# A matrix product with layer norm: the first quarter opened over four k tiles only, its sums put aside, and B's first pieces on a second queue

## The chip, the cores and the metric

The kernel runs on one core of one Trainium2 chip. A core has TensorE (PE, the matrix unit, with its weight loads shown as PEld), VectorE (DVE), ScalarE (ACT), GpSimd (POOL) and SyncE (SP), which run their own instruction lists in order and wait for each other by semaphores. Transfers are asked for by a queue (SP's, ScalarE's or GpSimd's) and done by 16 DMA engines. Matmul results go to PSUM, which holds eight banks of 128 partitions x 512 float32; everything else on the core lies in SBUF.

The metric is the device time of one execution in microseconds (us). Before the change it was 251.15 us, the median of three runs (250.21, 251.15, 252.37).

## The reference

```python
# a: 2048 x 2048, b: 2048 x 2048, gamma, beta: 2048, all float32; eps = 1e-5
x = np.matmul(a, b)
mean = np.mean(x, axis=-1, keepdims=True)
var = np.var(x, axis=-1, keepdims=True)
normalized = (x - mean) / np.sqrt(var + eps)
return (gamma * normalized + beta).astype(np.float32)
```

Each output row is normed over all 2048 columns, so a row can be finished only when all its columns are summed.

## The kernel before

**Tiles.** The 2048 rows of A are 16 row tiles of 128, the contraction is 16 k tiles of 128 (four chunks of four), and the columns are four quarters of 512. One matmul takes a 128 x 128 piece of A, transposed, as weights and a 128 x 512 piece of B; 16 of them, one per k tile, add up one bank: a row tile's quarter. There are 16 x 4 x 16 = 1024 matmuls (`mm`, line 86). Inputs are cast from float32 to float16 by VectorE; B stays in SBUF for the whole run.

**Opening.** The first R = 7 row tiles are worked on together while the input arrives. Pieces of 256 KB come in the order of the list `arrivals`: for chunk 0, A of row 0, B of k tile 0, A of row 1, B of k tile 1 and so on, then A of rows 4 to 6; for each later chunk, A of two rows and then a B tile. `load_piece` (lines 178 to 196) issues each on SP's queue into half of a staging buffer (tag `st`, six buffers of 512 KB) and has VectorE cast it. `turn` (lines 214 to 222) transposes a row's chunk on TensorE, four transposes of 128 x 128 per row, into one PSUM bank (two rows share a bank from chunk 1 on), and ScalarE copies the result to the tile `at`. `emit` hands out matmuls of quarter 0 between the transposes, as their A and B become known, and `filler` (line 212) puts in matmuls on zeros. Quarter 0's seven sums stay in seven banks over all four chunks, which leaves the eighth for transposes.

**First and second quarter.** Lines 280 to 284 finish quarter 0 row by row: ScalarE copies a bank to the row's tile `x` and VectorE takes its statistics (`evacuate`, lines 91 to 97). Then quarter 1 of all seven rows runs with the k tile outermost (lines 286 to 293), its last four k tiles row by row. B's remaining quarters come by `load_b2` (lines 198 to 203) in pieces of two k tiles, 512 KB, which `bring` places between the other work. VectorE runs its list in the order written, so where a `bring` stands sets what its cast waits behind.

**The rest.** From line 359 rows go one by one: rows 0 to 6 have quarters 2 and 3 left, rows 7 to 15 all four. When a row's last quarter is in, `stats` makes mean and root, and `queue_norm` puts the row's norm into `backlog` in two pieces of two quarters; `drain` places pieces between the evacuations. The norm is two VectorE passes per quarter (lines 112 and 118), then a store on SP's queue (line 124). A of rows 7 to 15 is loaded with a cast on GpSimd's queue (line 305), behind a copy (`gate`, line 276) that waits for the last B tile, and transposed by a DMA that SP issues at row i for row i + 5 (line 365). The last row has a shortened tail (`finish_row`).

Which tile uses which buffer follows from pools: `st` has six buffers, `a16` (A cast, not yet transposed) three, `at` four pairs of rows, `x` seven rows, and `ps` the eight PSUM banks. A new tile waits until the old one in its buffer has been read for the last time.

Of the kernel before, what the change touches and what calls it, by code (L numbers as in the profile page):

```python
# [9 lines left out]
FP32 = mybir.dt.float32  # L10
FP16 = mybir.dt.float16
AluOp = mybir.AluOpType
# [4 lines left out]
def kernel(  # L17
# [9 lines left out]
    nc = tc.nc  # L27
    P = 128
    M, K = a.shape
    K2, N = b.shape  # L30
    assert K == K2
    n_mt = M // P
    n_kt = K // P
    NB = 512
    n_nb = N // NB
    NH = N // 2
    KC = 4
    KW = KC * P
    n_kc = n_kt // KC
    R = 7  # L40
    early, e_cap, p_cap = 4, 3, 7
    n_row = n_mt - R
    assert n_kt % KC == 0 and n_nb == 4 and R % 2 == 1 and n_row >= 5

    if isinstance(eps, bass.AP):
        eps_ap, eps_val = eps, None
# [20 lines left out]
    b16 = bpool.tile([P, n_kt, N], FP16)  # L67

    pair = {}
    xs = [None] * n_mt  # L70
    bnst = [None] * n_mt
# [8 lines left out]
    def at(i):  # L80
        return pair[i // 2][:, i % 2]

    def mm(i, q, kt, first, last):
        if (i, q) not in acc:
            acc[i, q] = bank(f"acc{i}_{q}")
        nc.tensor.matmul(  # L86
            acc[i, q], at(i)[:, kt, :], b16[:, kt, ds(q * NB, NB)],
            start=first, stop=last,
        )

    def evacuate(i, q):
        if xs[i] is None:
            xs[i] = xpool.tile([P, N], FP32, tag="x", name=f"x{i}")
            bnst[i] = stat.tile([P, n_nb, 6], FP32, tag="bnst", name=f"bnst{i}")
        qs = ds(q * NB, NB)
        nc.scalar.copy(xs[i][:, qs], acc[i, q])  # L96
        nc.vector.bn_stats(bnst[i][:, q, :], xs[i][:, qs])  # L97
# [33 lines left out]
    def queue_norm(i, mv, sq):  # L131

        got = {}

        def piece(q0):
            def run():
                centre(i, q0, mv)
                centre(i, q0 + 1, mv)
                if q0 == 0:
                    got["rstd"] = inv(i, sq)  # L140
                scale(i, q0, got["rstd"])
                scale(i, q0 + 1, got["rstd"])
# [20 lines left out]

    arrivals = []
    for i in range(KC):
        arrivals += [("a", i, 0), ("b", i)]
    arrivals += [("a", i, 0) for i in range(KC, R)]
    for c in range(1, n_kc):
        k0 = c * KC
        for j in range(KC):  # L170
            arrivals += [("a", i, c) for i in range(2 * j, min(2 * j + 2, R))]
            arrivals.append(("b", k0 + j))

    a16_of = {}
    fresh = {"st": 0, "a": 0}
    held = {}

    def load_piece(what):
        n = fresh["st"]
        if n % 2 == 0:  # L180
            held["st"] = stg.tile([P, 2, NB], FP32, tag="st", name=f"st{n // 2}")
        fresh["st"] += 1
        st = held["st"][:, n % 2, :]
        if what[0] == "a":
            _, i, c = what
            nc.sync.dma_start(st, a[ts(i, P), ts(c, KW)])  # L186
            m = fresh["a"]
            if m % KC == 0:
                held["a"] = a16p.tile([P, K], FP16, tag="a16", name=f"a16s{m // KC}")
            fresh["a"] += 1  # L190
            a16_of[i, c] = held["a"][:, ts(m % KC, KW)]
            nc.vector.tensor_copy(a16_of[i, c], st)  # L192
        else:
            k = what[1]
            nc.sync.dma_start(st, b[ts(k, P), 0:NB])  # L195
            nc.vector.tensor_copy(b16[:, k, 0:NB], st)  # L196

    def load_b2(k, q):
        st = stg.tile([P, 2, NB], FP32, tag="st", name=f"stb{q}_{k}")
        nc.sync.dma_start(  # L200
            st, b[ds(k * P, 2 * P), ds(q * NB, NB)].rearrange("(t p) n -> p t n", p=P))
        nc.vector.tensor_copy(b16[:, k:k + 2, ds(q * NB, NB)], st)  # L202
        return st

    for what in arrivals:
        load_piece(what)

    warm = bank("warm")

# [4 lines left out]
    def turn(rows, c):  # L214
        n = len(rows)
        t_ps = psum.tile([P, n, KC, P], FP16, tag="ps", name=f"tps{rows[0]}_{c}")
        for m, i in enumerate(rows):
            for j in range(KC):
                nc.tensor.transpose(t_ps[:, m, j, :], a16_of[i, c][:, ts(j, P)], ident)  # L219
        i0 = rows[0]  # L220
        nc.scalar.copy(  # L221
            pair[i0 // 2][:, ds(i0 % 2, n), ds(c * KC, KC), :], t_ps)

    left = {i: n_kt for i in range(R)}
    queue, own = [], []
    turned, landed, here = set(), set(), set()

    def emit(n):
        for _ in range(min(n, len(queue))):
            i, kt = queue.pop(0)  # L230
            mm(i, 0, kt, left[i] == n_kt, left[i] == 1)
            left[i] -= 1

    gaps = {("a", 0, 0): (12, 3), ("a", 1, 0): (3, 2), ("a", 2, 0): (0, 2)}
    for what in arrivals:
        if what[0] == "b":
            k = what[1]
            now = [(i, k) for i in range(R) if (i, k // KC) in turned]
            new = {i for i, _ in own}
            queue += [x for x in now if x[0] not in new] + own  # L240
            queue += [x for x in now if x[0] in new]
            own = []
            landed.add(k)
            continue
        _, i, c = what
        here.add((i, c))
        if c == 0:
            rows = [i]
            if i < early:
                queue += own  # L250
                own = []
                emit(len(queue))
        else:
            mate = i ^ 1
            if mate < R and (mate, c) not in here:
                continue
            rows = sorted([i, mate]) if mate < R else [i]
        before, after = gaps.get(what, (0, 0))
        filler(before)
        turn(rows, c)  # L260
        filler(after)
        if c > 0:
            emit(p_cap)
        elif i >= early:
            emit(e_cap)
        queue += own
        turned |= {(r, c) for r in rows}
        own = [(r, k) for r in rows for k in sorted(landed) if k // KC == c]
    later = [(k, q) for q in range(1, n_nb) for k in range(0, n_kt, 2)]

    def bring(n):
        for _ in range(n):
            k, q = later.pop(0)
            st = load_b2(k, q)
            if not later:
                nc.gpsimd.tensor_copy(gate, st[:, 0, 0:1])  # L276

    queue += own
    queue.sort()
    for p in range(R):  # L280
        emit(left[p])
        bring(1)
        evacuate(p, 0)
    bring(n_kt - R)

    for kt in range(n_kt - KC):
        for p in range(R):
            mm(p, 1, kt, kt == 0, False)
    for p in range(R):
        for kt in range(n_kt - KC, n_kt):  # L290
            mm(p, 1, kt, False, kt == n_kt - 1)
        bring(1)
        evacuate(p, 1)
    bring(len(later))
    nc.sync.dma_start(gamma_b, gamma.unsqueeze(0).to_broadcast([P, N]))
    nc.sync.dma_start(beta_b, beta.unsqueeze(0).to_broadcast([P, N]))
    if eps_ap is not None:
# [58 lines left out]
                xs[i][:, qs], xs[i][:, qs], rstd, w[q], AluOp.mult, AluOp.add)  # L356
            store(i, q, 1)

    for i in range(n_mt):
        last = i == n_mt - 1  # L360
        t = i + 5
        if R <= t < n_mt:
            if t % 2 == 0:
                new_pair(t // 2)
            nc.sync.dma_start_transpose(at(t), a16[t])
        for q in range(2 if i < R else 0, n_nb):
            for kt in range(n_kt):
                mm(i, q, kt, kt == 0, kt == n_kt - 1)
            if last and q == n_nb - 1:
                break  # L370
            evacuate(i, q)
            if q < n_nb - 1:
                drain(1)
            if last:
                scaled(i, q)
        if last:
            drain(len(backlog))
            finish_row(i)
        else:
            mv, sq = stats(i)  # L380
            queue_norm(i, mv, sq)
            drain(1)


# [33 lines left out]
```

## Time and profile before

| | us |
|---|---|
| median of three runs | 251.15 |
| the profiled run's own time | 251.07 |
| its span | 249.30 |
| TensorE busy | 240.3 (96%) |
| VectorE busy | 171.5 (69%) |
| ScalarE busy | 57.3 (23%) |
| of 40 equal slices of the span, DMA at over 9 tenths busy | the first 70 us, but for the first slice |
| bytes moved by DMA | 52.65 MB |

The page gives, for each engine, its busy time; a table of 40 slices; the chain of work that ended last; and groups of instructions by line, with the mean duration of one and what ended the idle time before them. In a row of the timeline the first number is the start in us from the span's start, the second the duration of the group, and `x4` the number of instructions. `SPq` is SP's queue, that is, the instruction that issues a transfer, not the transfer. Matmuls are pipelined: one of 512 columns is shown with 379 ns on average, but they start 216 ns apart where nothing waits.

Durations used later, of one instruction: A and B casts of 128 x 512 take 427 ns, casts of 128 x 1024 take 695 ns, `bn_stats` 688 ns, ScalarE's copy of a bank 590 ns, its copy of a double transpose about 1.01 us, the two norm passes 744 and 747 ns.

### The profile page before, as it was taken

Reading aid. Unit: us, or ns where it says so; the run is one execution under the profiler, and the core shown is the slowest. Engines: PE = TensorE matmul, PEld = TensorE weight load, DVE = VectorE, ACT = ScalarE, POOL = GpSimd, SP = SyncE. Lnnn points to the kernel's source line nnn. Section 1 sums busy time; section 2 is a strip of 40 time slices with the busy share of each in tenths; the row PEclk is TensorE's granted clock in tenths of the full one; section 3 lists DMA queues with packets and bytes.
Section 4 is the critical chain, followed back from the end, with each engine's and each line's share of the span. In section 5 each row is a group of like instructions: output and inputs, shape, how many; then the busy total and the mean of one; then the engine's idle time right before and its main releaser. Section 6 shows DMA issues by size and latency. Waiting matters only on the chain.

```text
span 249.3 us, 3072 instructions
## 1 busy us (share of the span) xinstructions
PE 240.3 (96%) x1172; PEld 110.4 (44%) x1172; DVE 171.5 (69%) x315; ACT 57.3 (23%) x101; POOL 6.1 (2%) x15
## 2 busy tenths in 40 slices
PE   8898999999999999999999999999999999999982
PEld 2454554444444444444444444444444444444430
DVE  1465565954979999999949194765749292846873
ACT  2353547000523122211212111212121120212100
POOL 0000000000030000000000000000000000000000
PEclk9999999999999999999999999999999999999996
DMA  5999999999999899999999987090402222130404
GB/s 143 321 359 379 337 350 383 387 387 387 387 398 208 254 212 182 194 252 254 239 146 310 301 213 191 0 252 3 168 0 91 80 84 84 41 127 3 170 0 170
DMA packets 38087, 52.65 MB, mean 211 GB/s; under 512 B 20532, under 2 KB 20532, under 8 KB 37816
## 3 DMA queue, kind: packets, MB, share of 16 engines
q1 hardware_dynamic: 36776, 47.73, 59.0%
q0 software_dynamic: 1296, 4.72, 12.2%
q8 instruction: 9, 0.15, 0.2%
q14 instruction: 6, 0.05, 0.1%
HBM read 35.67 MB, written 16.78 MB: 210 GB/s over the span
## 4 chain that ended last, share of the span: by engine, by line
PE 87%; DMA 8%; SPq 1%; DVE 1%; issue 0%; ACT 0%
PE acc L86 85%; DMA st<-in_a_dram 5%; DMA st<-in_b_dram 3%; PE tps L219 1%; SPq L186 1%; PE w L345 1%; SPq L195 1%; DVE x L355 0%; DVE bnst L329 0%; DVE x L332 0%; DVE a16s L192 0%; PE nm_ps L340 0%; DVE mv L103 0%; ACT lead L341 0%; DVE nm L337 0%
## 5 line engine op out<-in xcount | busy, mean ns | idle before, releaser
L86 PE MATMUL acc<-b,at 128*128 128x512 f16 x1024 | 224.1, 379 | 0.1
L86 PEld LDWEIGHTS <-at 128*128 128x128 f16 x1024 | 99.4, 98 | 118.0 <-ACT at L221 1.4
L97 DVE BATCH_NORM_STATS2 bnst<-x 128x6 f32<-128x512 f32 x63 | 43.4, 688 | 43.4 <-ACT x L96 43.4
L96 ACT COPY x<-acc 128x512 f32<-128x512 f32 x63 | 36.3, 590 | 133.3 <-PE acc L86 131.9
L118 DVE SCALAR_TENSOR_TENSOR x<-x,rstd,beta_b 128x512 f32<-128x512 f32 x61 | 43.1, 747 | 0.5
L112 DVE SCALAR_TENSOR_TENSOR x<-x,mv,gamma_b 128x512 f32<-128x512 f32 x60 | 42.1, 744 | 0.0
L202 DVE CAST b<-stb 128x1024 f16<-128x1024 f32 x24 | 16.7, 695 | 8.2 <-DMA stb<-in_b_dram 7.5
L192 DVE CAST a16s<-st 128x512 f16<-128x512 f32 x28 | 12.0, 427 | 12.4 <-DMA st<-in_a_dram 12.3
L221 ACT COPY at<-tps 128x512 f16<-128x512 f16 (+1 forms) x19 | 15.0, 788 | 22.1 <-PE tps L219 22.1
L219 PE MATMUL tps<-ident,a16s 128*128 128x128 f16 x112 | 10.2, 220 | 2.1 <-DVE a16s L192 2.1
L219 PEld LDWEIGHTS <-a16s 128*128 128x128 f16 x112 | 7.8, 98 | 7.9 <-DVE a16s L192 3.5
L212 PE MATMUL warm<-zeros 128*128 128x512 f16 x30 | 10.0, 479 | 1.2 <-DVE zeros L153 1.2
L196 DVE CAST b<-st 128x512 f16<-128x512 f32 x16 | 6.8, 427 | 5.8 <-DMA st<-in_b_dram 5.6
L107 ACT ACTIVATE sq<-ve 128x1 f32<-128x1 f32 x16 | 3.3, 203 | 28.0 <-DVE ve L105 28.0
L305 POOL DMA_DIRECT2D a<-in_a_dram x9 | 4.9, 549 | 63.1 <-DMA at<-a 63.1
L212 PEld LDWEIGHTS <-zeros 128*128 128x128 f16 x30 | 3.3, 116 | 5.2 <-issue 2.8
L103 DVE BATCH_NORM_AGGREGATE mv<-bnst 128x2 f32<-128x24 f32 x16 | 4.2, 264 | 0.6
L105 DVE TENSOR_TENSOR ve<-mv,eps_t 128x1 f32<-128x1 f32 x16 | 2.6, 160 | 0.5
L128 DVE RECIPROCAL rstd<-sq 128x1 f32<-128x1 f32 x16 | 2.5, 156 | 0.0
L276 POOL COPY gate<-stb 128x1 f32<-128x1 f32 x1 | 0.7, 706 | 69.9 <-DMA stb<-in_b_dram 69.9
L345 PE MATMUL w<-gb,lead 2*128 2x512 f32 x4 | 2.0, 613 | 0.3 <-ACT lead L341 0.3
L322 DVE TENSOR_TENSOR x<-x,gamma_b 128x512 f32<-128x512 f32 x3 | 2.1, 691 | 0.1
(22 smaller groups left out, 10.1 us busy)
## 6 DMA issues: line engine op xcount, KB each, us to landing
out_dram<-x SPq DMA_DIRECT2D x30, 512.0 KB, 5.6
stb<-in_b_dram SPq DMA_DIRECT2D x24, 512.0 KB, 7.4
st<-in_a_dram SPq DMA_DIRECT2D x28, 256.0 KB, 6.0
a<-in_a_dram POOLq DMA_DIRECT2D x9, 512.0 KB, 8.4
st<-in_b_dram SPq DMA_DIRECT2D x16, 256.0 KB, 5.8
gamma_b<-in_gamma_dram SPq DMA_DIRECT2D x1, 1024.0 KB, 9.4
beta_b<-in_beta_dram SPq DMA_DIRECT2D x1, 1024.0 KB, 11.4
out_dram<-x SPq DMA_DIRECT2D x4, 256.0 KB, 2.8
```

The lines of the kernel that those rows point to most:

```text
L86: nc.tensor.matmul(acc[i, q], at(i)[:, kt, :], b16[:, kt, ds(q * NB, NB)], start=first, stop=last,)
L96: nc.scalar.copy(xs[i][:, qs], acc[i, q])
L97: nc.vector.bn_stats(bnst[i][:, q, :], xs[i][:, qs])
L112: nc.vector.scalar_tensor_tensor(xs[i][:, qs], xs[i][:, qs], mv[:, 0:1], gamma_b[:, qs], AluOp.subtract, AluOp.mult)
L118: nc.vector.scalar_tensor_tensor(xs[i][:, qs], xs[i][:, qs], rstd, beta_b[:, qs], AluOp.mult, AluOp.add)
L192: nc.vector.tensor_copy(a16_of[i, c], st)
L196: nc.vector.tensor_copy(b16[:, k, 0:NB], st)
L202: nc.vector.tensor_copy(b16[:, k:k + 2, ds(q * NB, NB)], st)
L212: nc.tensor.matmul(warm if to is None else to, zeros[:, 0:P], zeros, start=True, stop=True)
L219: nc.tensor.transpose(t_ps[:, m, j, :], a16_of[i, c][:, ts(j, P)], ident)
L221: nc.scalar.copy(pair[i0 // 2][:, ds(i0 % 2, n), ds(c * KC, KC), :], t_ps)
L305: nc.gpsimd.dma_start(a16[i], a[ts(i, P), :])
```

## The change

Quarter 0 is summed over chunk 0 only (k tiles 0 to 3), with `stop` at the fourth. ScalarE copies these seven sums into quarter 0 of the rows' `x` tiles, and the banks are free. Then quarter 1 is summed over all 16 k tiles, with A's chunks 1 to 3 transposed in between, and after it quarter 0 over k tiles 4 to 15 in new banks. VectorE adds the bank to what was put aside and takes the statistics.

The order of the loads follows: after chunk 0 come, per chunk, quarter 1's B in pieces of two k tiles and A's next chunk in pieces of two rows (`load_a2`, 512 KB, one cast; row 6 alone stays 256 KB). Quarter 0's B of k tiles 4 to 15 comes after that. Chunk 0's four B pieces are issued by ScalarE's queue, its A pieces by SP's. The filler counts differ: 9 and 3 around row 0's transposes (12 and 3 before), 1 and 2 around rows 1 and 2 (3 and 2, 0 and 2 before), 3 and 1 around row 3, and 3 ahead of row 4's.

In the row-by-row part, rows 0 to 2 do quarter 2 first, all three, then quarter 3, each with its norm; from row 3 on the order is as before. A's DMA transposes are issued for row i + 4, starting at row 3; `n_first` is 3.

```diff
+    def load_a2(i, c):
+        st = stg.tile([P, 2, NB], FP32, tag="st", name=f"sta{i}_{c}")
+        nc.sync.dma_start(
+            st, a[ds(i * P, 2 * P), ts(c, KW)].rearrange("(t p) k -> p t k", p=P))
+        for m in (0, 1):
+            a16_room(i + m, c)
+        nc.vector.tensor_copy(held["a"][:, ds(i % KC, 2), :], st)
+
+    def load_b1(k):
+        st = half_stage()
+        nc.scalar.dma_start(st, b[ts(k, P), 0:NB])
+        nc.vector.tensor_copy(b16[:, k, 0:NB], st)
...
     for what in arrivals:
-        load_piece(what)
+        (load_a1(what[1], 0) if what[0] == "a" else load_b1(what[1]))
+    for c in range(n_kc):
+        for h in (0, 1):
+            load_b2(c * KC + 2 * h, 1)
+            if c + 1 < n_kc:
+                load_pair(2 * h, c + 1)
+                load_pair(2 * h + 1, c + 1)
...
-    gaps = {("a", 0, 0): (12, 3), ("a", 1, 0): (3, 2), ("a", 2, 0): (0, 2)}
+    gaps = {0: (9, 3), 1: (1, 2), 2: (1, 2), 3: (3, 1), 4: (3, 0)}
...
-    later = [(k, q) for q in range(1, n_nb) for k in range(0, n_kt, 2)]
+    later = [(k, 0) for k in range(KC, n_kt, 2)]
+    later += [(k, q) for q in range(2, n_nb) for k in range(0, n_kt, 2)]
...
-    for p in range(R):
-        emit(left[p])
-        bring(1)
-        evacuate(p, 0)
-    bring(n_kt - R)
-
-    for kt in range(n_kt - KC):
+    for p in range(R):
+        emit(KC - done[p])
+        xs[p] = xpool.tile([P, N], FP32, tag="x", name=f"x{p}")
+        bnst[p] = stat.tile([P, n_nb, 6], FP32, tag="bnst", name=f"bnst{p}")
+        nc.scalar.copy(xs[p][:, 0:NB], acc.pop((p, 0)))
+    spots = {(h, p): 2 * h + m for h in (0, 1) for m, p in enumerate((2, 5))}
+    for h in (0, 1):
         for p in range(R):
-            mm(p, 1, kt, kt == 0, False)
+            for kt in (2 * h, 2 * h + 1):
+                mm(p, 1, kt, kt == 0, False)
+            if (h, p) in spots:
+                turn(pairs[spots[h, p]], 1)
+    for kt in range(KC, n_kt - KC):
+        for p in range(R):
+            mm(p, 1, kt, False, False)
+        turn(pairs[kt % KC], kt // KC + 1)
     for p in range(R):
         for kt in range(n_kt - KC, n_kt):
             mm(p, 1, kt, False, kt == n_kt - 1)
         bring(1)
         evacuate(p, 1)
-    bring(len(later))
+    bring(len(later) - 4)
+    for kt in range(KC, n_kt - KC):
+        for p in range(R):
+            mm(p, 0, kt, kt == KC, False)
+    for p in range(R):
+        for kt in range(n_kt - KC, n_kt):
+            mm(p, 0, kt, False, kt == n_kt - 1)
+        nc.vector.tensor_tensor(
+            xs[p][:, 0:NB], acc[p, 0], xs[p][:, 0:NB], AluOp.add)
+        nc.vector.bn_stats(bnst[p][:, 0, :], xs[p][:, 0:NB])
+        bring(min(1, len(later)))
...
-    for i in range(n_mt):
+    for q in (2, 3):
+        for i in range(n_first):
+            quarter(i, q)
+            evacuate(i, q)
+            if q == 3:
+                close(i)
+    for i in range(n_first, n_mt):
         last = i == n_mt - 1
-        t = i + 5
+        turn_ahead(i + 4)
         for q in range(2 if i < R else 0, n_nb):
```

More of the change, by code (lines that the diff above doesn't have):

```diff
@@ L41 @@
     early, e_cap, p_cap = 4, 3, 7
-    n_row = n_mt - R
-    assert n_kt % KC == 0 and n_nb == 4 and R % 2 == 1 and n_row >= 5
+    n_first = 3
+    assert n_kt % KC == 0 and n_nb == 4 and R % 2 == 1 and n_mt > R > n_first
     if isinstance(eps, bass.AP):
@@ L165, with half_stage @@
     for i in range(KC):
[L166 to L172, printed above, removed]
+        arrivals += [("a", i), ("b", i)]
+    arrivals += [("a", i) for i in range(KC, R)]
     a16_of = {}
-    fresh = {"st": 0, "a": 0}
+    fresh = {"st": 0}
     held = {}
-    def load_piece(what):
+    def half_stage():
         n = fresh["st"]
@@ L182, in load_piece, with a16_room, load_a1 @@
         fresh["st"] += 1
[L183 to L196, printed above, removed]
+        return held["st"][:, n % 2, :]
+    def a16_room(i, c):
+        if i % KC == 0:
+            held["a"] = a16p.tile([P, KC, KW], FP16, tag="a16", name=f"a16s{i}_{c}")
+        a16_of[i, c] = held["a"][:, i % KC, :]
+    def load_a1(i, c):
+        st = half_stage()
+        nc.sync.dma_start(st, a[ts(i, P), ts(c, KW)])
+        a16_room(i, c)
+        nc.vector.tensor_copy(a16_of[i, c], st)
+    def load_a2(i, c):
[6 more added lines that the diff above has]
+    def load_b1(k):
+        st = half_stage()
+        nc.scalar.dma_start(st, b[ts(k, P), 0:NB])
+        nc.vector.tensor_copy(b16[:, k, 0:NB], st)
     def load_b2(k, q):
@@ L203, in load_b2, with load_pair @@
         return st
-    for what in arrivals:
-        load_piece(what)
+    pairs = [list(range(i, min(i + 2, R))) for i in range(0, R, 2)]
+    def load_pair(j, c):
+        if len(pairs[j]) == 2:
+            load_a2(pairs[j][0], c)
+        else:
+            load_a1(pairs[j][0], c)
+    for what in arrivals:
+        (load_a1(what[1], 0) if what[0] == "a" else load_b1(what[1]))
[5 more added lines that the diff above has]
+                load_pair(2 * h + 1, c + 1)
     warm = bank("warm")
@@ L222, in turn @@
             pair[i0 // 2][:, ds(i0 % 2, n), ds(c * KC, KC), :], t_ps)
-    left = {i: n_kt for i in range(R)}
     queue, own = [], []
-    turned, landed, here = set(), set(), set()
+    turned, landed = set(), set()
     def emit(n):
@@ L230, in emit @@
             i, kt = queue.pop(0)
-            mm(i, 0, kt, left[i] == n_kt, left[i] == 1)
-            left[i] -= 1
-    gaps = {("a", 0, 0): (12, 3), ("a", 1, 0): (3, 2), ("a", 2, 0): (0, 2)}
+            done[i] += 1
+            mm(i, 0, kt, done[i] == 1, done[i] == KC)
+    done = [0] * R
+    gaps = {0: (9, 3), 1: (1, 2), 2: (1, 2), 3: (3, 1), 4: (3, 0)}
     for what in arrivals:
@@ L237 @@
             k = what[1]
-            now = [(i, k) for i in range(R) if (i, k // KC) in turned]
+            now = [(i, k) for i in sorted(turned)]
             new = {i for i, _ in own}
@@ L244 @@
             continue
[L245 to L258, printed above, removed]
+        i = what[1]
+        if i < early:
+            queue += own
+            own = []
+            emit(len(queue))
+        before, after = gaps.get(i, (0, 0))
         filler(before)
-        turn(rows, c)
+        turn([i], 0)
         filler(after)
-        if c > 0:
-            emit(p_cap)
-        elif i >= early:
+        if i >= early:
             emit(e_cap)
         queue += own
-        turned |= {(r, c) for r in rows}
-        own = [(r, k) for r in rows for k in sorted(landed) if k // KC == c]
-    later = [(k, q) for q in range(1, n_nb) for k in range(0, n_kt, 2)]
+        turned.add(i)
+        own = [(i, k) for k in sorted(landed)]
+    queue += own
+    queue.sort()
+    later = [(k, 0) for k in range(KC, n_kt, 2)]
+    later += [(k, q) for q in range(2, n_nb) for k in range(0, n_kt, 2)]
     def bring(n):
@@ L276, in bring @@
                 nc.gpsimd.tensor_copy(gate, st[:, 0, 0:1])
-    queue += own
-    queue.sort()
     for p in range(R):
-        emit(left[p])
-        bring(1)
-        evacuate(p, 0)
-    bring(n_kt - R)
-    for kt in range(n_kt - KC):
-        for p in range(R):
-            mm(p, 1, kt, kt == 0, False)
+        emit(KC - done[p])
[4 more added lines that the diff above has]
+    for h in (0, 1):
+        for p in range(R):
+            for kt in (2 * h, 2 * h + 1):
[6 more added lines that the diff above has]
+        turn(pairs[kt % KC], kt // KC + 1)
     for p in range(R):
@@ L357, in finish_row, with quarter, close, turn_ahead @@
             store(i, q, 1)
-    for i in range(n_mt):
-        last = i == n_mt - 1
-        t = i + 5
+    def quarter(i, q):
+        for kt in range(n_kt):
+            mm(i, q, kt, kt == 0, kt == n_kt - 1)
+    def close(i):
+        mv, sq = stats(i)
+        queue_norm(i, mv, sq)
+        drain(1)
+    def turn_ahead(t):
         if R <= t < n_mt:
@@ L365 @@
             nc.sync.dma_start_transpose(at(t), a16[t])
+    for q in (2, 3):
[5 more added lines that the diff above has]
+    for i in range(n_first, n_mt):
+        last = i == n_mt - 1
+        turn_ahead(i + 4)
         for q in range(2 if i < R else 0, n_nb):
-            for kt in range(n_kt):
-                mm(i, q, kt, kt == 0, kt == n_kt - 1)
+            quarter(i, q)
             if last and q == n_nb - 1:
@@ L379 @@
         else:
-            mv, sq = stats(i)
-            queue_norm(i, mv, sq)
-            drain(1)
+            close(i)
 _INS = ['a', 'b', 'gamma', 'beta', 'eps']
```

## The prediction

> **What bounds the kernel now.** I read first the chain of work that ended last, merged in order of time, because it says where the end is made.
>
> ```profile
> 23.91 0.44 DVE a16s L192
> 24.35 0.05 issue
> 24.40 0.40 PE tps L219 x4
> ...
> 38.44 201.17 PE acc L86 x932
> 239.61 0.02 issue
> 239.63 0.71 DVE bnst L329
> ```
>
> From 38.44 us on TensorE is the chain: 932 matmuls in 201.17 us, 0.2158 us each, no wait among them. Before 24.40 us the chain hangs on loads of A. So time can only be won or lost ahead of 38.44, or by breaking the solid stretch. Behind the last matmul (239.61) lie 9.69 us to the end of the span (249.30), and 1.77 us more to the profiled run's 251.07. That run is 0.08 us under the median of 251.15, so a forecast against one stands for the other.
>
> TensorE's timeline shows what the opening loses:
>
> ```profile
> 14.71 0.39 PE L219 MATMUL tps<-ident,a16s 128*128 128x128 f16 x4
> 14.94 0.81 PE L86 MATMUL acc<-b,at 128*128 128x512 f16 x3
> ...
> 19.35 0.40 PE L219 MATMUL tps<-ident,a16s 128*128 128x128 f16 x4
> 20.13 0.40 PE L219 MATMUL tps<-ident,a16s 128*128 128x128 f16 x4 [0.38 <-DVE a16s L192]
> ...
> 23.39 0.39 PE L219 MATMUL tps<-ident,a16s 128*128 128x128 f16 x4
> 24.40 0.40 PE L219 MATMUL tps<-ident,a16s 128*128 128x128 f16 x4 [0.61 <-DVE a16s L192]
> ```
>
> Each row here is a start, a duration and a group; idle time ahead of it stands in brackets. The group at 14.71 is row tile 6's first chunk; call its end, 14.94, the turning point. 15 matmuls lie before it (1+3+5+3+3 in the timeline), so 77 lie between it and 38.44. 77 x 0.2158 = 16.62 us. 21 groups of four transposes remain, 0.225 us each from start to next start (30.11 to 30.33, 14.71 to 14.94): 4.7 us. Together 21.3 of 23.5 us: **2.2 us are waiting**, 1.35 of it in the two places shown (19.35 and 23.39, a second row's A late).
>
> **The opening, part by part.** Matmuls and transposes are as many as before: behind the turning point again 1009 x 0.2158 = 217.74 and 4.7, that is 222.45 us plus whatever waiting s is left. The turning point again has 15 matmuls ahead of it. So the sum is: turning point + 222.45 + s + 9.69 + 1.77.
>
> *s.* Before, a chunk of 2.75 MB (11 pieces of 256 KB) brought 28 matmuls. After, the 28 matmuls of quarter 1 over k tiles 0 to 3 need only 1 MB more of B while the next A comes, so work is in hand. The stream's rate I take from the casts, which follow landing: row 6's first piece is cast at 13.80, and the fourth B tile of the last quarter at 66.08.
>
> ```profile
> 13.80 0.43 DVE L192 CAST a16s<-st 128x512 f16<-128x512 f32 x1 [0.25 <-DMA st<-in_a_dram]
> ...
> 66.08 0.69 DVE L202 CAST b<-stb 128x1024 f16<-128x1024 f32 x1
> ```
>
> Between them 73 pieces of 256 KB: 0.716 us each, 366 GB/s. After, 13 pieces lie between row 6's first piece and the B tile of k 4: landed 23.1, cast (0.69) 23.8; TensorE wants it 13 + 28 matmuls and 7 groups behind the turning point, 10.43 us, at 24.9 to 25.4. Cover: 1.1 to 1.6 us. Per chunk the stream takes 11 x 0.716 = 7.88 us, TensorE 7.62, so cover falls by 0.26 each, and the last two B tiles are both wanted within 0.43 us: there it is gone, by up to 0.4 us. Pieces of 512 KB help. In the table of stretches (busy time of each engine, then clock, DMA share, GB/s) loads by such pieces ran at 386 to 388 GB/s, loads by 256 KB at 325 to 374:
>
> ```profile
> 25.00:30.00 5.00, 5.00 (x37) 2.75 (x35) 3.00 (x8) 2.87 (x3) 0.00 (x0) 1.00 0.96 325
> ...
> 50.00:55.00 5.00, 5.00 (x25) 2.28 (x24) 2.65 (x4) 0.00 (x0) 0.00 (x0) 1.00 1.05 387
> ```
>
> Both rows of an A pair now come from one transfer and one cast (0.69 instead of two of 0.43), which removes the case "second row late". Bounds for s: 0, and 2.2 as now. I take **0.5**, nearer the covered end.
>
> *The turning point.* Now eight B and A pieces are issued by SP alone:
>
> ```profile
> 2.61 0.43 SPq L186 DMA_DIRECT2D st<-in_a_dram  x1
> 3.08 0.66 SPq L195 DMA_DIRECT2D st<-in_b_dram  x1
> 3.78 0.86 SPq L186 DMA_DIRECT2D st<-in_a_dram  x1
> 4.68 0.66 SPq L195 DMA_DIRECT2D st<-in_b_dram  x1
> 5.38 3.68 SPq L186 DMA_DIRECT2D st<-in_a_dram  x5
> ```
>
> The eighth is out at 5.34; with four on each queue at 0.43 us it is out at about 2.6. The DMA share was only 0.48 in 2.0 to 3.0 us, and rates fell to 205 to 311 GB/s in 9.0 to 11.5, so both holes may close: row 6's piece would land up to 1.1 us earlier (B's first piece at 6.64 plus nine at 0.67 = 12.7). Against it: the ninth load, free at 5.38 now, waits after for B's first piece to land (6.64). And the new order has its own floor. Nine fillers end at 1.19 + 9 x 0.43 = 5.0; row 0's transposes and three more slow fillers end at about 6.5 to 6.7; from there to the turning point come 15 matmuls, 13 fillers and 6 groups, 28 x 0.216 + 1.35 = 7.4: not before 14.0. With arrivals unchanged the same list gives 14.95 (the last wait is row 4's cast at 12.91). Bounds 14.0 and 14.95; I take **14.5**. ScalarE's four issues (0.43 each) delay its table load (1.28 us at 0.74) to about 3.8; its first copy was wanted at 6.73 and is now at about 5.3, so they are hidden; without that cover they would cost up to 1.7.
>
> The Trainium skill, "DMA: Bandwidth & Descriptors", section "Issuing engines are not separate DMA queues", says that issuing from several engines saves only the sequencer's time, since all run on the same 16 engines. By that alone the turning point would stay at 14.95 and the forecast at 249.4.
>
> *Putting sums aside.* ScalarE's seven copies of the first quarter now stand right behind the turning point: seven took 3.52 us (at 40.20 us now), so they run from 0.6 to 4.1 us behind it, while TensorE, which fills quarter 1 there, asks for these banks from 3.2 to 6.3 us behind it in the same order; hidden by about 2 us. Later seven VectorE additions are new. No row shows one; from L322's 0.69 (both operands in SBUF) and L332's 0.74 (one in PSUM) I take 0.74.
>
> **Where the cover is thin.** A first-quarter bank is now freed by that addition, and VectorE's program puts the casts of 18 B tiles ahead of row 0's addition, the last being the tile cast at 66.08 now. At the old rate the addition ends at 66.08 + 0.69 + 0.74 = 67.5. TensorE has one free bank for row 0's quarter 2 and wants the added one for row 1 when 784 matmuls are left: last matmul minus 169.2 us. With turning point 14.5 and s 0.5 the last matmul ends at 237.45, so it wants the bank at 68.25: **0.75 us of cover**. The next additions come 2.1 us apart (cast 0.69, addition 0.74, statistics 0.69) and are wanted 3.45 apart: only the first matters.
>
> **Behind it.** Rows 0 to 2 do quarter 2 first, so the first norm starts 13.8 instead of 6.9 us into that phase; VectorE, busy 9.8 of 10 us in 80 to 120, then runs some 5 us behind, now about 3. That holds ScalarE's copies behind a square root, but seven banks at 3.45 us are 24 us of cover. SP is in order: A's transpose for row 7 stands behind three stores, the third about 28 us into the phase, and lands 7.5 us later; row 7 is wanted at 48. Hidden by 12 us. The tail stays.
>
> **Sum.** 14.5 + 222.45 + 0.5 + 9.69 + 1.77 = **248.9 us**, 2.2 less than 251.07 (0.9%).
>
> **Rivals.**
> 1. *Gain eaten, 250.2 to 251.2.* TensorE's clock. The fillers run 0.43 us apart up to 6.3, then 0.216. With three fewer in front, a late first piece leaves TensorE idle and the slow pitch may last another 3 us, which halves what is done: +1.5 us on the turning point. Or the new order hides nothing and s stays at 2: 14.95 + 2.0 gives 250.9. For: the pitch changed only after 5.1 us of fillers without a gap. Against: the new list stays nearly dense to 6.7.
> 2. *Slower, the stream of B becomes the bound at row 1's quarter 2.* If the stream from 13.5 on is slower than 359 GB/s (19.1 MB by 66.8 us) the addition comes late and the solid stretch breaks; under 345 GB/s (addition at 70.4) the kernel is slower than before. At 325, the worst window above, it ends at 73.8: 73.8 + 169.2 + 9.69 + 1.77 = 254.5. For: one of six staging buffers is held for row 6's odd piece, and casts stand behind statistics in 41 to 51 us. Against: 512 KB pieces ran at 387 with the same interleaving.
> 3. *All of it, 247.9.* Turning point 14.0, s 0.
>
> The Trainium skill, "TensorE: Matmul & The Clock Gate", section "Part 1: The HAM clock gate", has the clock freed after a busy window of some 3.4 us, free-running; the slow pitch until 6.3 agrees, and by it the switch could move by one window between runs.
>
> **Numbers.** Forecast case (247.9 to 249.7, with rival 3 at its low end): 0.60; rival 1: 0.23; rival 2: 0.17, most of it between 251.2 and 254.5. A measurement of this kernel tells about 1% from no change, that is under 248.6 or over 253.7. Under 248.6: half of the forecast case and a little scatter, 0.32. Over 253.7: the far part of rival 2 and what I have missed, 0.13; the rest, 0.55, lies between. Range 247.6 to 252.2.
>
> **What would show it.** Right: row 6's first transposes end near 14.5; transposes of eight 0.45 us apart with no idle before them; solid matmuls to the end; row 0's addition before about 68. Wrong: idle before a matmul of quarter 2 that names the addition; a DMA rate under 360 in 15 to 65 us; fillers 0.43 apart beyond 7 us.

## The result and the profile after

The changed kernel takes 252.62 us (median of 20 runs, 251.11 to 253.88), beside 251.76 us for the kernel before (20 runs, 250.08 to 253.74): ratio **1.0042 [1.0023, 1.0062]**. It is 0.4% slower, where 0.9% faster was forecast. The profiled execution has a span of 249.4 us and a time of 251.50 us. That is 1.1 us under its median, so the profile shows less than what the median lost. Of the 20 executions the ten quicker (251.1 to 252.4 us) had a mean granted clock of 0.989 to 0.994 and the ten longer (252.8 to 253.9) one of 0.984 to 0.989; the profile is of a quicker one, so what the longer ones lost beyond it is not shown.

The chain of work that ended last, of the changed kernel, in order of time (start, duration, what):

```profile
1.19 8.29 DMA st<-in_a_dram
9.50 0.44 DVE a16s L189
9.99 0.61 PE tps L239 x4
10.60 0.52 PE warm L232 x2
...
14.70 0.86 PE warm L232 x4
...
43.15 196.85 PE acc L86 x912
240.01 0.02 issue
240.03 0.71 DVE bnst L363
```

The solid stretch is there, 912 matmuls 0.2158 us apart, and its last matmul ends at 240.01 us (239.61 before). From 9.99 us on TensorE is the chain without a break; ahead of that there is one transfer, the A piece of row 1, whose cast begins at 9.50. Pieces marked `warm` are fillers on zeros: twelve of them stand in this chain, 12 x 0.216 = 2.6 us.

TensorE's timeline of the changed kernel (start, duration, line, operation, count; idle time ahead in brackets):

```profile
1.19 4.02 PE L232 MATMUL warm<-zeros 128*128 128x512 f16 x9 [1.19 <-DVE zeros L153]
6.63 0.61 PE L239 MATMUL tps<-ident,a16s 128*128 128x128 f16 x4 [1.42 <-DVE a16s L189]
7.03 1.49 PE L232 MATMUL warm<-zeros 128*128 128x512 f16 x3
...
9.99 0.61 PE L239 MATMUL tps<-ident,a16s 128*128 128x128 f16 x4 [0.61 <-DVE a16s L189]
...
17.14 0.39 PE L239 MATMUL tps<-ident,a16s 128*128 128x128 f16 x4
17.36 4.26 PE L86 MATMUL acc<-b,at 128*128 128x512 f16 x19
21.46 0.61 PE L239 MATMUL tps<-ident,a16s 128*128 128x128 f16 x8
```

The turning point (the end of row 6's first transposes, as in the prediction) is **17.36 us**; before it was 14.94, and 14.5 was forecast. Behind it no row of the timeline has idle time: 43.15 + 196.85 - 17.36 - 222.45 = 0.2 us of waiting, where there were 2.2 before. So the change won 2.0 us behind the turning point and lost 2.4 ahead of it.

VectorE's timeline names what was late. First the kernel before, then the changed one; a cast follows the landing of its piece:

```profile
4.58 0.43 DVE L192 CAST a16s<-st 128x512 f16<-128x512 f32 x1 [3.37 <-DMA st<-in_a_dram]
...
7.33 0.43 DVE L192 CAST a16s<-st 128x512 f16<-128x512 f32 x1 [0.24 <-DMA st<-in_a_dram]
```

```profile
6.15 0.43 DVE L189 CAST a16s<-st 128x512 f16<-128x512 f32 x1 [4.94 <-DMA st<-in_a_dram]
6.49 0.42 DVE L202 CAST b<-st 128x512 f16<-128x512 f32 x1
9.50 0.43 DVE L189 CAST a16s<-st 128x512 f16<-128x512 f32 x1 [2.59 <-DMA st<-in_a_dram]
```

Row 0's A is cast at 6.15 us instead of 4.58, row 1's at 9.50 instead of 7.33. B's first piece is not late (6.49; it was 6.64). The table of stretches, again before and then after (busy time of each engine with its instructions, granted clock, DMA share, GB/s):

```profile
2.00:5.00 3.00, 3.00 (x8) 1.06 (x7) 0.42 (x1) 0.02 (x1) 0.00 (x0) 1.00 0.73 141
5.00:9.00 4.00, 3.97 (x22) 1.72 (x20) 1.61 (x5) 0.92 (x2) 0.00 (x0) 1.00 1.00 372
```

```profile
2.00:5.00 3.00, 3.00 (x8) 0.91 (x6) 0.00 (x0) 1.28 (x1) 0.00 (x0) 1.00 0.77 131
5.00:9.00 4.00, 2.58 (x10) 0.98 (x9) 0.76 (x2) 0.58 (x1) 0.00 (x0) 1.00 0.84 275
```

From 2 to 5 us the DMA engines were about as busy as before (0.77 beside 0.73) and moved a little less, 131 GB/s instead of 141; from 5 to 9 us they were less busy (0.84 beside 1.00) and moved 275 instead of 372. The issues, in the timelines of SP and ScalarE (from the first's start to the last's end, count):

```profile
0.74 9.26 SPq L187 DMA_DIRECT2D st<-in_a_dram  x7
...
0.74 2.68 ACTq L201 DMA_DIRECT2D st<-in_b_dram  x4
3.46 1.28 ACT L241 ACT_TABLE_LOAD   x1 [3.46 <-issue]
```

The 9.26 us are not seven long issues. SP's first four end at 3.40 us, the longest of them 1.28 us; then SP stands still. Its timeline from 3.5 to 9.6 us, and the row of its waits (total, times, longest):

```profile
6.31 1.05 SPq L187 DMA_DIRECT2D st<-in_a_dram  x2
```

```profile
SPq L187 <- DMA st<-in_b_dram: 5.2, 2, 2.9
```

So all eight pieces of rows and k tiles 0 to 3 were asked for by 3.42 us, where the eighth was out at 5.34 before. The A pieces of rows 4 to 6 had to wait until pieces of B had landed; the last of them is asked for at 9.68.

### The profile page after: what moved, and what is told of

It is laid out like the page before. It is cut to its first block, busy times and chain, and to the rows that moved or that the text cites. A ratio compares the mean times of both kernels' runs of the same rounds, so it can differ in the third digit from the quotient of the medians.

```text
span 249.4 us, 3055 instructions
## 1 busy us (share of the span) xinstructions
PE 240.9 (97%) x1175; PEld 111.0 (45%) x1175; DVE 172.4 (69%) x307; ACT 57.0 (23%) x101; POOL 5.6 (2%) x15
## 3 DMA queue, kind: packets, MB, share of 16 engines
q0 software_dynamic: 1296, 4.72, 11.4%
## 4 chain that ended last, share of the span: by engine, by line
PE 93%; DMA 3%; DVE 1%; issue 0%; SPq 0%; ACT 0%
PE acc L86 89%; DMA st<-in_a_dram 3%; PE tps L239 3%; PE warm L232 1%; PE w L379 1%; DVE x L389 0%; DVE bnst L363 0%; DVE x L366 0%; DVE a16s L189 0%; PE nm_ps L374 0%; SPq L187 0%; DVE mv L103 0%; ACT lead L375 0%; DVE nm L371 0%; DVE ve L105 0%
## 5 line engine op out<-in xcount | busy, mean ns | idle before, releaser
L208 DVE CAST b<-stb 128x1024 f16<-128x1024 f32 x30 | 20.7, 690 | 13.9 <-DMA stb<-in_b_dram 13.6
L232 PE MATMUL warm<-zeros 128*128 128x512 f16 x33 | 11.6, 483 | 1.2 <-DVE zeros L153 1.2
L197 DVE CAST a16s<-sta 128x1024 f16<-128x1024 f32 x9 | 6.2, 694 | 7.9 <-DMA sta<-in_a_dram 7.9
L189 DVE CAST a16s<-st 128x512 f16<-128x512 f32 x10 | 4.2, 424 | 8.6 <-DMA st<-in_a_dram 8.6
L325 DVE TENSOR_TENSOR x<-acc,x 128x512 f32<-128x512 f32 x7 | 4.8, 681 | 0.0
```

What stands on the lines that cost most here:

```text
L197: nc.vector.tensor_copy(held["a"][:, ds(i % KC, 2), :], st)
L232: nc.tensor.matmul(warm if to is None else to, zeros[:, 0:P], zeros, start=True, stop=True)
```

## The experiments

All kernels below compute the whole reference. Two questions were asked: which part of the change costs the time, and why. B 0 stands for B's piece of k tile 0, A 0 for the chunk 0 piece of row 0. The table comes first; "2-5" and "5-9" are GB/s of the stretch table, "row 1's A" and "row 6's A" the start of those casts, and ratios are to the kernel before beside each run.

| kernel | 2-5 | 5-9 | row 1's A | row 6's A | turning point | span | ratio |
|---|---|---|---|---|---|---|---|
| before | 141 | 372 | 7.33 | 13.80 | 14.94 | 249.3 | 1 |
| after | 131 | 275 | 9.50 | 14.37 | 17.36 | 249.4 | 1.0042 [1.0023, 1.0062] |
| one queue | 150 | 346 | 6.83 | 14.38 | 15.47 | 247.5 | 0.9912 [0.9891, 0.9933] |
| old order, two queues | 134 | 310 | 7.80 | 14.79 | 15.89 | 251.1 | 1.0067 [1.0047, 1.0086] |
| B 0 and 1 on the second | 130 | 279 | 9.75 | 14.41 | 17.40 | 249.4 | 0.9986 [0.9959, 1.0012] |
| B 3 on the second | 228 | 299 | 7.07 | 13.82 | 16.39 | 248.4 | 0.9971 [0.9942, 1.0001] |
| row 2's A, B 2 on the second | 232 | 366 | 7.59 | 11.89 | 15.24 | 247.2 | 0.9897 [0.9857, 0.9938] |
| row 1's A, B 1 on the second | 228 | 341 | 7.05 | 12.75 | 14.77 | 246.8 | 0.9908 [0.9875, 0.9940] |
| four B on the second, 1 0 3 2 | 209 | 341 | 8.14 | 12.58 | 17.08 | 249.1 | 0.9988 [0.9951, 1.0025] |
| four B on the second, other buffers | 133 | 271 | 8.19 | 15.04 | 17.36 | 249.4 | 1.0055 [1.0022, 1.0087] |
| one queue, three A first | 232 | 317 | 7.58 | 12.38 | 15.30 | 247.3 | 0.9935 [0.9906, 0.9963] |
| two queues, few fillers | 126 | 283 | 9.58 | 14.38 | 16.75 | 249.4 | 0.9979 [0.9961, 0.9997] |
| one queue, few fillers | 147 | 358 | 7.02 | 13.90 | 16.72 | 248.7 | 0.9925 [0.9899, 0.9951] |
| row 2's A, B 2 on the second, few fillers | 230 | 358 | 7.55 | 12.30 | 13.82 | 245.8 | 0.9889 [0.9851, 0.9926] |

### The two parts apart

The new order with B's first pieces back on SP's queue:

```diff
-        nc.scalar.dma_start(st, b[ts(k, P), 0:NB])
+        nc.sync.dma_start(st, b[ts(k, P), 0:NB])
```

> The changed kernel with chunk 0's four B pieces on SP's queue again, between the A pieces; nothing else differs. Theory Q (the second queue slows the first arrivals: row 0's A cast at 6.15 instead of 4.58, row 1's at 9.50 instead of 7.33): arrivals go back to those of the kernel before, row 6's first transposes end at about 14.95 instead of 17.36, and the ratio to the kernel before is about 0.993. Theory N (the new order alone, its staging and its waits, makes the arrivals late, whatever the queue): row 1's A is cast at 9 us or later and the ratio stays at about 1.004.

Measured: 249.24 us, ratio 0.9912 [0.9891, 0.9933], 0.9% faster than before. Its casts of A 0, B 0 and A 1, the end of its turning point in TensorE's timeline, and its chain:

```profile
4.72 0.43 DVE L189 CAST a16s<-st 128x512 f16<-128x512 f32 x1 [3.51 <-DMA st<-in_a_dram]
5.92 0.43 DVE L202 CAST b<-st 128x512 f16<-128x512 f32 x1 [0.78 <-DMA st<-in_b_dram]
6.83 0.43 DVE L189 CAST a16s<-st 128x512 f16<-128x512 f32 x1 [0.48 <-DMA st<-in_a_dram]
```

```profile
15.47 4.26 PE L86 MATMUL acc<-b,at 128*128 128x512 f16 x19
```

```profile
13.49 0.40 PE tps L239 x4
...
41.26 196.85 PE acc L86 x912
```

The turning point is 15.47. Behind it, 41.26 + 196.85 - 15.47 - 222.45 = 0.2 us are waiting. **The new order alone wins about what was forecast for the whole change; the second queue takes it away**: row 1's A comes 2.7 us later with it, and the turning point 1.9. That the size agrees is in part luck. The turning point is still 1.0 us behind the 14.5 of the forecast, and 0.3 us less waiting and a tail shorter by 0.3 make up part of it. The other half is the old order with two queues (an edit of the kernel before):

```diff
-            nc.sync.dma_start(st, b[ts(k, P), 0:NB])
+            (nc.scalar if k < KC else nc.sync).dma_start(st, b[ts(k, P), 0:NB])
```

> The kernel before with its first four B pieces on ScalarE's queue; nothing else differs. Theory Q: row 1's A is cast near 9.5 here too. With few fillers behind row 1's transposes the opening can catch up: row 6's first transposes end at 15.3 to 15.5 instead of 14.94, and the ratio to the kernel before is 1.001 to 1.003. Theory N: arrivals as before, ratio 1.000.

Measured: 252.86 us, ratio 1.0067 [1.0047, 1.0086]; more than was expected. Row 0's A is cast at 6.59, and the long wait is for row 2's A (11.04), not for row 1's (7.80, where 9.5 was expected). The turning point is 15.89, 0.95 us later than before, and waiting behind it is 40.44 + 201.17 - 15.89 - 222.45 = 3.3 us instead of 2.2. So the second queue costs time under either order: 0.7% under the old one, 1.3% under the new one (1.0042 over 0.9912).

### Fillers and the pitch of the matmuls

In the changed kernel twelve fillers stand in the chain. They were taken out, first with two queues, then with one (`gaps` and, in the second, the edit of the one-queue kernel):

```diff
-    gaps = {0: (9, 3), 1: (1, 2), 2: (1, 2), 3: (3, 1), 4: (3, 0)}
+    gaps = {0: (9, 3), 1: (1, 0)}
```

> The changed kernel, both queues, without the twelve fillers behind row 1's first transposes. Theory F (once row 1's A is late, these fillers are on the path, 12 x 0.216 = 2.6 us, because the chain of waits names them): limited by arrivals, row 6's first transposes end at about 15.4 instead of 17.36, ratio to the kernel before about 0.996. Rival C (the fillers only fill waiting; without them TensorE keeps its slow pitch of 0.43 us for longer): the end moves by less than 0.7 us and the ratio stays above 1.001.

> The changed kernel with the B pieces on SP's queue and without the twelve fillers. Theories Q and F: arrivals as before, row 6's first transposes end at 14.7 to 14.95, hardly earlier than with the fillers on one queue (there they fit into the waiting), ratio to the kernel before 0.992 to 0.993. Rival C: a longer slow pitch makes it later than with the fillers, ratio 0.996 or more.

With two queues: 251.01 us, ratio 0.9979 [0.9961, 0.9997], 0.6% better than the changed kernel, each against the kernel before. But the turning point moved only from 17.36 to 16.75, not by the 2 us that were expected, and its timeline says why:

```profile
10.06 0.40 PE L239 MATMUL tps<-ident,a16s 128*128 128x128 f16 x4 [1.77 <-DVE a16s L189]
...
12.22 2.35 PE L86 MATMUL acc<-b,at 128*128 128x512 f16 x5
14.36 0.81 PE L239 MATMUL tps<-ident,a16s 128*128 128x128 f16 x8
```

TensorE waits 1.77 us, and about two us later five matmuls take 2.35 us: the slow pitch of 0.43 is back. With one queue the same shows at once: 249.33 us, ratio 0.9925 [0.9899, 0.9951], no better than with the fillers, though row 6's A came at 13.90 instead of 14.38.

```profile
13.07 0.56 PE L239 MATMUL tps<-ident,a16s 128*128 128x128 f16 x4 [1.40 <-DVE a16s L189]
13.42 1.49 PE L86 MATMUL acc<-b,at 128*128 128x512 f16 x3
...
15.13 1.49 PE L86 MATMUL acc<-b,at 128*128 128x512 f16 x3
```

Three matmuls take 1.49 us here and 0.81 in the kernel before, and the turning point is 16.72. This profiled execution is 1.2 us above the median of its kernel, so the slow pitch need not come in every one. The fillers thus do two things: they cost their time where TensorE is behind its data, and without them the pitch can fall. With two queues taking them out won back about half of the 1.3% that the second queue costs; with one queue there was nothing to win.

### Which pieces run side by side

Why is the second queue slow? If merely more pieces in flight or a second queue were at fault, fewer pieces on it should cost in proportion. Three kernels put other pieces of chunk 0 there: B of k tiles 0 and 1; B of k tile 3 alone; and row 2's A with B of k tile 2. The edits of the changed kernel:

```diff
+        (nc.scalar if k < 2 else nc.sync).dma_start(st, b[ts(k, P), 0:NB])
...
+        (nc.scalar if k == 3 else nc.sync).dma_start(st, b[ts(k, P), 0:NB])
...
+        (nc.scalar if c == 0 and i == 2 else nc.sync).dma_start(st, a[ts(i, P), ts(c, KW)])
+        (nc.scalar if k == 2 else nc.sync).dma_start(st, b[ts(k, P), 0:NB])
```

> The changed kernel with k tiles 0's and 1's B pieces alone on ScalarE's queue, k tiles 2 and 3 on SP's. Theory M: the first four pieces land two and two together, but fewer compete, since the later ones are issued by SP behind them: row 0's A cast at 5.2 to 6.2, row 1's at 7.3 to 8.5; row 6's first transposes end at 15.5 to 16.5, ratio 0.995 to 1.000. Theory I: row 0's A is cast at 4.7 as on one queue and k tile 0's B at 6.5 or later.

> The changed kernel with only k tile 3's B piece on ScalarE's queue, issued at 0.74 us though it is wanted last. Theory M: its 256 KB go ahead of pieces that are wanted sooner, so row 0's to row 2's pieces land up to 0.7 us later, and row 3's A and the pieces behind it, which SP issues about 0.7 us sooner, up to 0.7 us earlier; row 6's first transposes end between 14.8 and 15.6 (15.47 on one queue), ratio 0.989 to 0.994. Theory I: arrivals on SP's queue to row 2 as on one queue.

> The changed kernel with only row 2's A piece and k tile 2's B piece of chunk 0 on ScalarE's queue, the other six of the first eight on SP's. Theory M (what is in flight on the second queue takes turns with the first queue's pieces, so the first ones wait for bytes that are wanted later): row 0's and row 1's pieces are late again (row 0's A cast at 5.3 us or later, row 1's at 8 or later, against 4.72 and 6.83 on one queue), and the third pair is cast at about the same time as the first two. Theory I (only the start of ScalarE's queue is slow, the pieces on SP's are not touched): row 0's and row 1's pieces are cast as on one queue, to 0.3 us, and only the third pair is late. Ratio to the kernel before: M 0.995 to 1.000, I 0.991 to 0.995.

Measured: 0.9986 [0.9959, 1.0012], 0.9971 [0.9942, 1.0001] and 0.9897 [0.9857, 0.9938]. Two pieces on the second queue are as slow at the start as four (130 GB/s), or much faster than one queue (232), depending on which two. With B 0 and B 1 there, the A pieces came later than expected (row 1's at 9.75, 7.3 to 8.5 expected). The stretches of the third kernel:

```profile
2.00:5.00 3.00, 2.81 (x8) 0.91 (x6) 0.43 (x1) 0.94 (x1) 0.00 (x0) 1.00 0.88 232
5.00:9.00 4.00, 2.57 (x16) 1.06 (x16) 1.60 (x5) 1.08 (x2) 0.00 (x0) 1.00 1.02 366
```

A second queue is therefore no harm in itself. That the gain would be small here was wrong: row 6's A came at 11.89, 2.5 us earlier than in the changed kernel. What the slow starts seem to have in common is that A of row tile i and B of k tile i are asked for side by side. A and B have the same shape, so these two pieces lie at the same offset in their tensors. The next kernels tested this reading. Row 1's pair on the second queue, as above with 1 for 2; then all four B pieces on the second queue as in the change, only asked for in the order 1, 0, 3, 2; then in the order 0 to 3 again, but each staged in its neighbour's half of the staging buffer, so that the destinations differ and the sources do not; last, everything on SP's queue, with A of rows 0, 1 and 2 ahead of the first B piece. In the last three VectorE's casts stay in the old order. The core of these edits:

```diff
+        (nc.scalar if c == 0 and i == 1 else nc.sync).dma_start(st, a[ts(i, P), ts(c, KW)])
+        (nc.scalar if k == 1 else nc.sync).dma_start(st, b[ts(k, P), 0:NB])
...
+    for k in (1, 0, 3, 2):
+        nc.scalar.dma_start(staged["b", k], b[ts(k, P), 0:NB])
...
+        staged[what if what[0] == "a" else ("b", what[1] ^ 1)] = half_stage()
...
+    for what in [("a", 0), ("a", 1), ("a", 2), ("b", 0), ("b", 1), ("a", 3), ("b", 2), ("b", 3)]:
+        i = what[1]
+        nc.sync.dma_start(staged[what], a[ts(i, P), 0:KW] if what[0] == "a" else b[ts(i, P), 0:NB])
```

> The changed kernel with row 1's A piece and k tile 1's B piece on ScalarE's queue, the other six of the first eight on SP's. Theory P (the second queue helps as long as the two queues do not read row tile i and k tile i side by side: 232 GB/s in 2 to 5 us with row 2's pair on it, 131 with all four B pieces): a rate over 200 GB/s in 2 to 5 us, row 0's A cast at 4.5 to 4.9, row 6's by 12.5. Theory E (what is wanted early must not be on ScalarE's queue): row 1's A cast at 8.5 or later, rate under 170.

> The changed kernel, all four B pieces on ScalarE's queue, but asked for in the order of k tiles 1, 0, 3, 2, so that A's row tile i and B's k tile i, which lie at equal offsets in their tensors, are not read side by side; casts in the order as before. Theory P: rate in 2 to 5 us over 200 GB/s (131 with the order 0, 1, 2, 3), row 0's A cast before 5.2 instead of 6.15; k tile 0's B, second on its queue, not before 6.5. Theory E: rate under 160, row 0's A cast at 5.8 or later.

> The changed kernel, all four B pieces on ScalarE's queue in the order 0, 1, 2, 3, but k tile i's piece is staged in the buffer beside the A piece of the neighbouring row instead of the one beside row i's. Theory D (the cost is the two queues writing the two halves of one staging buffer at the same time): rate in 2 to 5 us over 200 GB/s, row 0's A cast before 5.2. Theories P and E: as in the changed kernel, rate about 131, row 0's A cast at 5.8 to 6.6, ratio 1.002 to 1.006.

> The changed kernel with all first eight pieces on SP's queue, asked for in the order A0, A1, A2, B0, B1, A3, B2, B3, so that A's row tile i and B's k tile i are two or more pieces apart; casts in the order as before. It asks whether the 141 to 150 GB/s of one queue in 2 to 5 us has the same cause as the 131 of two. Theory P1 (pieces at equal offsets of A and B in flight together are slow on one queue too): rate in 2 to 5 us over 190, row 6's A cast at 12.0 to 13.0 instead of 14.38, ratio 0.985 to 0.991. Theory P2 (one queue is held by its own rate of asking at the start, the pairing costs only where two queues ask at once): rate 130 to 165, k tile 0's B, fourth now, cast at 7.0 or later, ratio 0.990 to 0.996.

Measured, first stretch each. Row 1's pair: 228 GB/s, ratio 0.9908 [0.9875, 0.9940]. Then B in the order 1, 0, 3, 2; B in other halves of the buffers; and one queue with A first:

```profile
2.00:5.00 3.00, 2.86 (x8) 0.91 (x6) 0.00 (x0) 1.28 (x1) 0.00 (x0) 1.00 0.81 209
5.00:9.00 4.00, 1.77 (x9) 0.78 (x10) 1.52 (x4) 0.59 (x1) 0.00 (x0) 0.85 0.99 341
9.00:12.00 3.00, 3.00 (x16) 1.52 (x15) 1.93 (x6) 0.59 (x1) 0.00 (x0) 0.63 1.04 382
```

```profile
2.00:5.00 3.00, 2.93 (x8) 0.91 (x6) 0.00 (x0) 1.28 (x1) 0.00 (x0) 1.00 0.82 133
```

```profile
2.00:5.00 3.00, 3.00 (x8) 1.06 (x7) 0.43 (x1) 0.03 (x1) 0.00 (x0) 1.00 0.74 232
```

With the same pieces on the same two queues, the order 1, 0, 3, 2 moves 209 GB/s where 0, 1, 2, 3 moves 131 (133 with the staging exchanged). With the same pieces on the same single queue, the order A A A B moves 232 where A B A B moves 150. **So the rate of the start goes with the order of the requests, and neither with the number of queues nor with the place in SBUF.** In the eight slow profiles (126 to 150 GB/s, the kernel before and the one-queue kernel among them) the first two requests are A 0 and B 0; in the six fast ones (209 to 232) A 0 goes out beside another piece or is followed by one of A. That the equal offsets are what makes this pair slow is only argued: with row 2's pair, row 1's pair or B 3 on the second queue, SP still asks for A 0, B 0, A 1 and B 1 one after the other, and the fast rate is then put down to the other queue's pieces running in between. No run puts another pair of equal offsets first, such as A 1 and B 1. Why equal offsets should be slow together is open; the profile shows no memory bank.

The Trainium skill, "DMA: Bandwidth & Descriptors", section "Latency and other measured facts", tells of slow copies at row pitches from 512 KiB up and calls conflicts between memory channels an inference; rows here are 8 KB apart, and no run here shows whether that is the same thing.

The slow start is not the whole of what the second queue costs. The one-queue kernel starts slowly too (150 GB/s) and wins 0.9%, and row 6's A is cast at the same time in both, 14.38 with one queue and 14.37 with two. By 12 us they have moved 2.70 and 2.60 MB. What differs is the early pieces: with two queues A 0 and B 0 come together (6.15 and 6.49, beside 4.72 and 5.92) and A 1 at 9.50 instead of 6.83, with some 7 us of TensorE's list, fillers included, behind it. Eight pieces asked for at once that share the engines would land like this; no run separates that from the slow start.

Early data did not always become time. B 3 alone on the second queue had 228 GB/s at the start, but row 2's A was cast at 10.46 (8.79 with one queue), the turning point was 16.39, and the ratio of 0.9971 missed the expected 0.989 to 0.994. The order 1, 0, 3, 2 gave only 0.9988 [0.9951, 1.0025]: B 0 was late (cast at 7.80), TensorE waited 1.68 us at 8.28, and the granted clock was 0.85 and then 0.63 in the rows above, with a turning point of 17.08. With one queue and A first (0.9935 [0.9906, 0.9963]) row 6's A came at 12.38, as expected of the pairing, but B 0 came at 7.24 and the fillers, now in the chain, held the turning point at 15.30, so the ratio fell where the other theory had it (0.990 to 0.996).

Last, the best arrival with few fillers: row 2's pair on the second queue and the short `gaps` line.

> The changed kernel with only row 2's A piece and k tile 2's B piece on ScalarE's queue (arrivals to row 6 were cast by 11.89 us there, TensorE was the bound from row 1's transposes on) and without the twelve fillers behind row 1's transposes. Theory F (these fillers are on the path as soon as data is there): row 6's first transposes end 2.3 to 2.6 us earlier, at 12.6 to 12.9 instead of 15.24, waiting behind that stays under 0.6 us, ratio to the kernel before 0.979 to 0.983. Rival C (without them the slow pitch comes back): matmuls behind 9 us 0.43 apart, ratio 0.986 or more.

Measured: 248.36 us, ratio **0.9889 [0.9851, 0.9926]**; the turning point is 13.82, not 12.6 to 12.9.

```profile
7.20 0.38 PE L86 MATMUL acc<-b,at 128*128 128x512 f16 x1 [1.06 <-DVE b L202]
...
9.26 0.81 PE L86 MATMUL acc<-b,at 128*128 128x512 f16 x3 [0.83 <-DVE b L202]
...
13.60 0.39 PE L239 MATMUL tps<-ident,a16s 128*128 128x128 f16 x4
13.82 4.26 PE L86 MATMUL acc<-b,at 128*128 128x512 f16 x19
```

It waits for B 0 and B 1, 1.06 and 0.83 us, and the pitch stays at 0.216; the ratio lies where rival C had it (0.986 or more), but not for rival C's reason. In its profile this kernel is 1.4 us ahead of the one with the fillers (245.8 against 247.2); the two ratios do not tell them apart. These two, row 1's pair and the three one-queue kernels beat both kernels of the case; their intervals overlap, so they can't be ranked.

## Why the prediction was wrong

**The step that failed is the turning point.** Bounds 14.0 and 14.95 were given, 14.5 was taken, 17.36 was measured: +2.86 us. The upper bound was "with arrivals unchanged", since the step held that with four pieces on each queue the holes in the transfers "may close". It took earlier issue for earlier landing. The issue did come earlier: eight pieces were out at 3.42 us, not 2.6, but not 5.34 either. The landing came later: the rate fell to 131 and 275 GB/s, and row 1's A is cast 2.2 us later than before. What the prediction held against itself, that a later load waits for B's first piece to land, came true and had no price in the sum: SP waited 5.2 us, and asked for row 6's A at 9.68 (6.83 in the one-queue kernel). The rows of that stretch already held a warning: a DMA share of 0.73 with 141 GB/s, beside 1.00 with 372 later, means engines that were busy for far less traffic, so a late request could not be all that was wrong.

The runs split the 2.86 us. With B back on SP's queue the turning point is 15.47, so 1.9 us go with the second queue. The other 1.0 us stays without it: the floor of 14.0 was not reached, and even the 14.95 of unchanged arrivals was missed, since row 4's A, the last wait named there, was cast at 13.01 and not at 12.48.

From row 1's transposes the list then ran as the floor was worked out: 14 matmuls and 12 fillers at 0.2158 and six groups at 0.225 are 6.96 us; from 9.99 to 17.36 are 7.37, and the other 0.4 is the slow pitch at the start of it. The rule of the Trainium skill weighed there, "Issuing engines are not separate DMA queues", points the right way in that a fast start needed no second queue (232 GB/s on one). By it alone the turning point stayed at 14.95; the runs show that which pieces go on the second queue, at the same filler list, moves it from 14.77 to 17.40.

**The waits behind the turning point** were sized well: s was 0.2 us (0.5 taken, bounds 0 and 2.2). The one-queue kernel shows that the order does this: its s is 0.2 as well.

**The thin cover held.** The first addition, by VectorE's timeline of the changed kernel:

```profile
66.54 0.69 DVE L208 CAST b<-stb 128x1024 f16<-128x1024 f32 x1 [0.66 <-DMA stb<-in_b_dram]
67.15 0.68 DVE L325 TENSOR_TENSOR x<-acc,x 128x512 f32<-128x512 f32 x1
```

It ends at 67.83 (67.5 forecast), and one takes 0.68 us (0.74 taken). TensorE, late itself, wanted the bank at 240.01 - 169.2 = 70.8. In the one-queue kernel, with an earlier TensorE:

```profile
65.03 0.68 DVE L325 TENSOR_TENSOR x<-acc,x 128x512 f32<-128x512 f32 x1
```

The addition ends at 65.71 and is wanted at 238.11 - 169.2 = 68.9. Cover was 3 us in both, where 0.75 was forecast, so rival 2, the stream as the bound, did not occur.

**What was costed at nothing** was nothing: ScalarE's first copy at 7.28 us lies far behind its table load (3.46 to 4.74); its seven copies of the sums put aside (3.53 us from 18.05) and the other order of the later phase leave the matmuls unbroken to the end. The tail took 9.39 us instead of 9.69, and what lies around the span 2.10 instead of 1.77.

The sum thus: 248.9 + 2.86 (turning point) - 0.3 (s) - 0.3 (tail) + 0.3 (around the span) = 251.5, the profiled run's time. **Rival 1** named a mechanism that took part, a late first piece that leaves TensorE idle and the slow pitch on (three fillers in 1.49 us at 7.03), but put it at 1.5 us and as a matter of the clock. In this profile it cost only the 0.4 us above, since ahead of 9.99 TensorE waited 0.61 us for row 1's A even so; whether it cost more in the longer executions is not shown. The one-queue kernel, with the same fillers, has no such wait ahead of row 0's transposes. No rival had the second queue making the first pieces late, which was the one that came.

## What to carry to other kernels

Issuing transfers earlier or on another queue changes which of them run side by side; look at the casts that follow each landing and at GB/s beside the DMA share before counting it as a gain, and try the order of requests first: here two orders on the same queues ran at 131 and 209 GB/s at the start. Then look at which piece TensorE waits for first: a faster start helps only if that piece is early. Where a change has two parts, run each alone: one here won 0.9%, the other lost more. Fillers that keep TensorE's pitch up are free only while the data they cover is late; when the arrivals move, count them again, and look whether the pitch survives without them.

## What the runs showed of the hardware that was not expected

- Where the first two requests of the kernel were 256 KB loads from equal offsets of two tensors of one shape (rows 8 KB apart), the loads ran at 126 to 150 GB/s from 2 to 5 us, in eight profiles; where the first request had another neighbour, at 209 to 232, in six. Both rates were seen with one queue and with two, and exchanging the staging buffers changed nothing (133). Why is open.
- Issues could become long at the slow start: beside 0.39 to 0.43 us for the first ones, the fourth load of each queue took 1.28 us in the changed kernel, and B 3 took 1.60 us on SP's queue where B 0 and B 1 were on the second.
- The slow pitch of 0.43 us came back after TensorE had waited 1.40 us (one queue, few fillers), 1.68 (B in the order 1, 0, 3, 2) and 1.77 (two queues, few fillers), and not after waits of 1.43 (one queue, three A first), 1.50 (B 3 on the second), 1.67 (two queues, few fillers, the wait ahead of row 0) and 1.69 us (other buffers). The length of one wait does not decide it. The granted clock in the rows does not always show the pitch: it was 1.00 from 5 to 9 us in the changed kernel, where three fillers took 1.49 us, and 0.85 and 0.63 where B was asked for in the order 1, 0, 3, 2.
